# A two-layer trunk of mLSTM heads and RG-LRU: xb of group 1 ahead of the out chunks, weight sums begun behind casts, the LRU's z behind the head's y, and a background grant of 1.2

## The chip, the core and the metric

The kernel runs on one core of one Trainium2 chip. The metric is the device time of one execution in microseconds (us); the lower, the better. Before the change it is 1487.85, the median of three runs (1487.43 to 1488.35).

## The reference

Two layers, each x + [y_a, y_b] W_out with u = rms_norm(x), x of 256 rows and 2048 columns, everything float32:

```python
u = rms_norm(x, norm_g)
qk, v, o, z_a, ig, fg, xb, z_b = split(u @ w_in)
qk = silu(causal_dwconv(qk, qk_conv)); q, k = split(qk)        # 8 heads, dk 128, dv 256
h = mlstm_chunkwise(q, k, v, ig + i_bias, log_sigmoid(fg + f_bias)) * sigmoid(o)
y_a = head_norm(h) * head_norm_g * silu(z_a)
xc = causal_dwconv(xb, lru_conv_w) + lru_conv_b
y_b = rg_lru(xc, w_a, b_a, w_x, b_x, lam) * silu(z_b)          # h_t = a_t h_(t-1) + u_t
x = x + concat(y_a, y_b) @ w_out
```

After the second layer follows a final rms_norm. The products with w_in (2048 x 12304) and w_out (4096 x 2048) are nearly all of the work on the matrix engine.

## The kernel before

**Groups, items, halves.** Each layer is worked in four groups g of two mLSTM heads and 512 LRU channels. An item is one product of a group: "in" with a kind (qk, v, o, z for the heads, xb and zb for the LRU), "gate" (the LRU's two gates) or "out" (512 columns of the product of the group before with w_out). `_sequence` writes the order of the items by hand, one layer after the other and group by group; an item has 1 to 4 units of 1 MB of weights, and a unit two halves of 128 x 1024. In what follows a half is called by item and group, such as o2 or zb1. Two items of groups 2 and 3 (PAIR: z of group 2 and o of group 3) are not multiplied in this way but by seven products of blocks and sums of blocks, 28 smaller "block" halves to a layer, strewn between the others.

**A half.** float32 products are made of float32r pieces: `prepare` casts a raw half to wH on ACT and subtracts it on DVE, wL = raw - wH; then PE runs twelve matmuls of 512 columns (x high by wH, x high by wL, x low by wH; block halves run six). The main loop goes over the halves: it prepares half n + 3 (AHEAD), emits the matmuls of half n, and pumps background work. wH and wL have four buffers each, so that a cast waits for the matmuls of the half four before it.

**Background work.** All else is written as generators in the list bg: each yields the price of what it has emitted, or "wait" to let the turn pass. `pump` runs them in their order until the credit of the step is spent. The grant per half is a fixed number, and a greater one (2.6) when more than two generators, beside those put aside, are in the list. Such work is recorded with V (DVE) and S (ACT), whose instructions are ordered behind the splits (DVE: the split before the newest; ACT: the newest cast). All engines run their instructions in the order in which they were emitted, but the scheduler may move what is not ordered. The generators that the change touches:

- `qk_post` (the queries and keys of a group): the product is transposed on its way through memory (blk, moved on SP's queue, fr on POOL's queue), joined to ch on ACT, then a convolution of four taps on DVE and ACT (qc, 4 x 4 instructions), a sigmoid, a product, and the split qks. It then makes scores (Pt), ps_n, the head norm, and so on, in later generators.
- `e_gen`: nG (a row of the gates) is written to memory by `gates_gen`, and nb is read back as a broadcast; E is formed from nb in four DVE instructions.
- `xb_post`: the same transposition for xb; the convolution xc and its split xcs, which the gate item multiplies (ps_gt). `gate_post`: the LRU's gates and scan, which end in the key "lru".
- `zb_post`: the transposed z_b, its sigmoid, y_b and its split (ybH, ybL); for group 3 of layer 0 `zb_post_c` does it by channels with no transposition. "hz" means that head h and z have been combined, "yT" that the head's y stands transposed.
- `out_chunk`: for groups 0 to 2 a staged product that POOL's queue adds to x_d in memory (accumulating DMA, st["gq"]).
- `block_sums`: makes sums of x (sums, sum_t) and, in `moved`, sums of weight blocks in memory: w_d begins as a copy on SP's queue, and further blocks are added to it by accumulating DMAs on POOL's queue, PACE steps apart; `load_block` reads it as rawb.

**Queues.** SP's queue carries the loads raw and rawb, the moved transpositions and the first w_d copies. POOL's queue carries fr, nb, x_d and the w_d adds.

**Lines.** 112 is the wrapper through which V and S record; 395 is `mm_a` (products with x or y), 840 the gate's matmuls, 940 to 946 `zb_post_c`, 1093 the add to w_d, 516 fr, 637 nb, 1149 to 1151 the block products, 1410 the pump.

Of the kernel before, what the change touches and what calls it, by code (L numbers as in the profile page):

```python
# [20 lines left out]
DEPTH = 2  # L21
# [20 lines left out]
def _sequence():  # L42
# [6 lines left out]
    for l in range(DEPTH):  # L49
        for g in range(NG):  # L50
            fill = [("out", l, g - 1, c) for c in range(4)] if g > 0 else []
            head = {0: ("o", "qk", "v"), 1: ("qk", "o", "v"), 2: ("qk", "o", "v")}.get(g, ("o", "v", "qk"))
            items = [("in", l, k, g) for k in head]
            at = 0 if ("z", g) in PAIR else 2
            items += fill[0:at] + [("in", l, "xb", g)] + fill[at:4]
            items += [("in", l, "z", g), ("gate", l, g)]
            items.insert(len(items) if g > 0 else -2, ("in", l, "zb", g))
            us = [u for it in items for u in units(it)]
            if l > 0 and g == 0:
                us[0:8] = [us[i] for i in (0, 4, 1, 5, 2, 6, 3, 7)]  # L60
            seq += us
# [36 lines left out]
def tile_trunk(ctx, tc, x, xt, par, gw, gb, ws, final_g, out):  # L98
# [165 lines left out]
    def order(ins, prev):  # L264
        tc.add_manual_dep(ins.ins, prev.ins.name,
                          mybir.DependencyInfo(mybir.DependencyClass.NoSync, mybir.DependencyReason.DATA),
                          reason="an order of the program")

    bg, aside = deque(), []
# [416 lines left out]
    def qk_post(l, g, acc):  # L686
        bg.append(e_gen(l, g))
        fr = to_channels(l, acc)

        def gen():  # L690
            for _ in range(LANDING):
                yield "wait"
            ch = joined(fr)
            yield 0.3
            qc = work.tile([P, 4, T], F32, tag="c4", name="qc", bufs=2)
            sg = work.tile([P, 4, T], F32, tag="sC", name="qsg")
            for ct in range(4):
                conv(ch, qc, ct, O_QKW + 4 * (8 * (ct % 2) + 2 * g + ct // 2), l, None)
                yield 1.2
            order(S.activation(out=sg, in_=qc, func=AF.Sigmoid), st["wH"])  # L700
            tt_(qc, qc, sg, ALU.mult)
            yield 1.2
            while ("aT", l) not in st:
                yield "wait"
            q = work.tile([P, 4, 2, T], F32R, tag="xcs", name="qks")
            S.copy(out=q[:, :, 0, :], in_=qc)
            tt_(q[:, :, 1, :], qc, q.bitcast(F32)[:, :, 0, :], ALU.subtract)
            yield 1.2
            for _ in range(3):
# [140 lines left out]
    def gate_post(l, g):  # L850
        ending = (l, g) == (DEPTH - 1, NG - 1)

# [41 lines left out]
    def zb_post(l, g, acc):  # L894
# [3 lines left out]
        def gen():  # L898
            for _ in range(LANDING - 3 if ending else FAR):
                yield "wait"  # L900
            while ("lru", l, g) not in st or ("hz", l, g) not in st:
                yield "wait"
# [21 lines left out]
    def zb_post_c(l, g, acc, s_):  # L924
# [11 lines left out]
        def gen():  # L936
# [6 lines left out]
            yield 0.2  # L943
            S.copy(out=yH[:, sl_, :], in_=zb[:, sl_, :])
            tt_(yL[:, sl_, :], zb[:, sl_, :], yH.bitcast(F32)[:, sl_, :], ALU.subtract)
            if s_ == 1:
# [22 lines left out]
    def out_chunk(l, g, c):  # L969
# [9 lines left out]
        def postfn():  # L979
            ps = acc()  # L980
            if g < NG - 1:
                stage = act.tile([P, 2, 512], F32, tag="stage", name="stage")
                S.copy(out=stage, in_=ps)
                st["gq"] = G.dma_start(out=xd[c], in_=stage, accum_op=ALU.add)
                return
            if c == 0:
# [37 lines left out]
    def block_sums(l):  # L1024
# [5 lines left out]
        def made(i, key, negated, p, q, pieces=1, after=None):  # L1030
            to, n = sums[i], 8 // pieces
            for k in range(pieces):
# [13 lines left out]
                for f in (difference,  # L1046
# [7 lines left out]
                    yield 1.2 / pieces + 0.1  # L1054
                    yield "wait"
                    if pieces == 1:
                        yield "wait"
                if pieces == 4:
# [26 lines left out]
    def weight_sums():  # L1085

        def moved(l, to, start, r, c, j, h):
            cs = slice(1024 * h, 1024 * h + 1024)
            src = block_unit(l, r, c, j)[:, cs]
            if start:  # L1090
                order(nc.sync.dma_start(out=wd[l][to][j][:, cs], in_=src), st["ld"])
            else:
                order(G.dma_start(out=wd[l][to][j][:, cs], in_=src, accum_op=ALU.add), st["gq"])
            for _ in range(PACE[l]):
# [286 lines left out]
    for n, hf in enumerate(order_):  # L1381
# [27 lines left out]
        if "from" not in hf:  # L1409
            pump(1.05 if sum(g not in aside for g in bg) <= 2 else 2.6)  # L1410
    drain()
# [94 lines left out]
```

## Time and profile before

| | value |
|---|---|
| median of 3 runs | 1487.85 us |
| the profiled execution, its own time | 1487.9 us |
| its span | 1486.1 us |
| bytes moved | 383.43 MB, mean 258 GB/s |
| matmuls, VectorE, ScalarE instructions | 6782, 1564, 1226 |

The span is the time from the first to the last instruction of the profiled execution; the rest of its time lies around it. In a row of the timeline stand the start, the duration, the engine, the line, the operation, output<-inputs, and in brackets the idle time of the engine before it with what ended it. A DVE or ACT instruction overlaps the next by about 0.1 us, so that the step from one start to the next, not the duration, is what it takes of the engine.

### The profile page before, as it was taken

What the parts mean: (1) busy time and instruction counts of PE and PEld (TensorE: products, weight loads), DVE (VectorE), ACT (ScalarE), POOL (GpSimd) and SP (SyncE); (2) the same over time, 40 slices, a digit from 0 to 9 for tenths busy, and PEclk for the clock granted to TensorE, in tenths of its full rate; (3) what the DMA queues carried; (4) which work ended last, traced back from release to release, by engine and by line L of the source; (5) the groups of instructions that cost most, each with busy time, mean ns of one, the idle gap of its engine ahead of it and who ended that gap; (6) DMA issues with size and microseconds to landing.
All of it is one profiled execution on the core that took longest, in us unless ns stands there. A gap on an engine that the chain in (4) does not pass through costs nothing.

```text
span 1486.1 us, 18768 instructions
## 1 busy us (share of the span) xinstructions
PE 1471.3 (99%) x6782; PEld 1226.2 (83%) x6782; DVE 1144.3 (77%) x1564; ACT 957.4 (64%) x1226; POOL 110.4 (7%) x186
## 2 busy tenths in 40 slices
PE   9999999999999999999999999999999999999997
PEld 7888888888888888888888787888888888888886
DVE  5788987788777676778867789867888776766785
ACT  7666865567655765558665577755667567655675
POOL 0020000100100001000000100000001000010002
PEclk9999999999999999999999999999999999999999
DMA  9867899998987998985886667698698668677783
GB/s 338 322 205 253 264 340 270 295 285 251 314 266 255 273 303 268 288 276 213 278 285 191 216 203 244 239 263 268 224 282 287 226 226 241 234 242 262 237 276 116
DMA packets 104045, 383.43 MB, mean 258 GB/s; under 512 B 11392, under 2 KB 31888, under 8 KB 84496
## 3 DMA queue, kind: packets, MB, share of 16 engines
q1 hardware_dynamic: 87536, 327.41, 63.0%
q0 software_dynamic: 13952, 50.35, 15.5%
q10 hardware_dynamic: 2464, 4.47, 0.8%
q8 instruction: 53, 0.87, 0.2%
q14 instruction: 40, 0.33, 0.1%
HBM read 344.95 MB, written 62.41 MB: 274 GB/s over the span
## 4 chain that ended last, share of the span: by engine, by line
PE 87%; DVE 5%; issue 3%; ACT 2%; DMA 2%; SPq 0%; POOL 0%; DVEq 0%; POOLq 0%; ACTq 0%
PE acc L395 73%; PE ps_gt L840 3%; DVE wL L112 2%; PE ps_b L1149 1%; PE ps_b L1150 1%; PE ps_b L1151 1%; PE acc L408 1%; ACT wH L112 1%; PE acc L1248 1%; PE acc L1246 1%; PE acc L1247 1%; DVE gate L112 1%; ACT L112 1%; DVE xc L112 0%; PE ps_g L568 0%
## 5 line engine op out<-in xcount | busy, mean ns | idle before, releaser
L395 PE MATMUL acc<-wH,x_s 128*128 128x512 f32 x2752 | 860.6, 390 | 0.6 <-ACT wH L112 0.6
L112 DVE TENSOR_TENSOR wL<-raw,wH 128x1024 fp32r<-128x1024 f32 (+1 forms) x500 | 598.3, 1203 | 244.9 <-ACT wH L112 243.5
L112 ACT CAST wH<-raw 128x1024 fp32r<-128x1024 f32 (+1 forms) x500 | 514.8, 1037 | 368.6 <-PE acc L395 304.0
L395 PEld LDWEIGHTS acc<-wH,x_s 128*128 128x128 f32 x2752 | 516.1, 188 | 108.0 <-ACT wH L112 1.9
L395 PE MATMUL acc<-wL,x_s 128*128 128x512 f32 x1376 | 534.7, 390 | 3.7 <-DVE wL L112 3.7
L395 PEld LDWEIGHTS acc<-wL,x_s 128*128 128x128 f32 x1376 | 258.4, 188 | 57.9 <-DVE wL L112 5.1
L395 PE MATMUL acc<-wH,ybL 128*128 128x512 f32 x224 | 87.3, 390 | 0.7 <-DVE ybL L112 0.7
L395 PE MATMUL acc<-wH,ybH 128*128 128x512 f32 x224 | 87.3, 390 | 0.0
L395 PE MATMUL acc<-wL,yaH 128*128 128x512 f32 x224 | 87.2, 389 | 0.0
L395 PE MATMUL acc<-wH,yaH 128*128 128x512 f32 x224 | 87.2, 389 | 0.0
L395 PE MATMUL acc<-wH,yaL 128*128 128x512 f32 x224 | 87.1, 389 | 0.0
L395 PE MATMUL acc<-wL,ybH 128*128 128x512 f32 x224 | 87.0, 389 | 0.0
L112 ACT ACT_TABLE_LOAD x60 | 77.0, 1283 | 10.6 <-DVE qc L112 5.3
L112 DVE TENSOR_TENSOR wL<-rawb,wH 128x1024 fp32r<-128x1024 f32 x56 | 68.5, 1223 | 7.7 <-ACT wH L112 6.6
L112 ACT CAST wH<-rawb 128x1024 fp32r<-128x1024 f32 x56 | 59.0, 1053 | 21.2 <-PE acc L395 11.2
L516 POOL DMA_DIRECT2D fr<-moved x34 | 18.9, 557 | 518.3 <-DMA moved<-blk 343.7
L112 DVE SCALAR_TENSOR_TENSOR qc<-ch,pars,qc 128x255 f32<-128x255 f32 (+2 forms) x96 | 42.8, 479 | 11.1 <-ACT qc L112 10.4
L395 PEld LDWEIGHTS acc<-wH,ybL 128*128 128x128 f32 x224 | 42.1, 188 | 9.9 <-DVE ybL L112 1.1
L395 PEld LDWEIGHTS acc<-wH,yaH 128*128 128x128 f32 x224 | 42.1, 188 | 8.7
L395 PEld LDWEIGHTS acc<-wH,yaL 128*128 128x128 f32 x224 | 42.0, 188 | 8.7
L395 PEld LDWEIGHTS acc<-wL,yaH 128*128 128x128 f32 x224 | 42.1, 188 | 8.6
L395 PEld LDWEIGHTS acc<-wH,ybH 128*128 128x128 f32 x224 | 42.0, 188 | 8.5
(222 smaller groups left out, 1607.6 us busy)
## 6 DMA issues: line engine op xcount, KB each, us to landing
raw<-in_ws_dram SPq DMA_DIRECT2D x152, 1024.0 KB, 6.6
raw<-in_ws_dram SPq DMA_DIRECT2D x190, 512.0 KB, 5.9
fr<-moved POOLq DMA_DIRECT2D x34, 512.0 KB, 6.1
moved<-blk SPq DMA_DIRECT2D x132, 128.0 KB, 2.9
w_d<-in_ws_dram POOLq DMA_DIRECT2D x32, 512.0 KB, 9.9
rawb<-w_d SPq DMA_DIRECT2D x32, 512.0 KB, 6.2
rawb<-in_ws_dram SPq DMA_DIRECT2D x24, 512.0 KB, 6.2
x_d<-stage POOLq DMA_DIRECT2D x24, 512.0 KB, 7.2
```

The lines of the kernel that those rows point to most:

```text
L112: ins = f(*a, **k)
L395: st["mm"] = PE.matmul(o, a_[:, kt, P * t : P * t + P], W[:, k], start=b, stop=z)
L408: PE.matmul(ps[:, ct, T * part : 2 * T], W[:, k, P * ct : P * ct + P], moving, start=first and k == 0 and part == 0, stop=last and k == 3 ...
L516: i0 = back.dma_start(out=fr.rearrange("p a c t i -> p a (c t i)"), in_=moved)
L840: PE.matmul(o, W[:, ib, jl], xs[:, ib, a, :], start=j == 0 and i == 0 and W is Hv and a == 0, stop=i == 1 and W is Lv, skip_group_check=True)
L1149: PE.matmul(box["b"], aH, Hv[:, k], start=opening and k == 0, stop=False, skip_group_check=True)
L1150: PE.matmul(box["b"], aH, Lv[:, k], start=False, stop=False, skip_group_check=True)
L1151: PE.matmul(box["b"], aL, Hv[:, k], start=False, stop=kp == 3 and k == 1, skip_group_check=True)
L1246: PE.matmul(o, yH[:, kt, tsl], Hv[:, k, cs], start=start and k == 0, stop=False)
L1247: PE.matmul(o, yH[:, kt, tsl], Lv[:, k, cs], start=False, stop=False)
L1248: PE.matmul(o, yL[:, kt, tsl], Hv[:, k, cs], start=False, stop=stop and k == 1)
```

## The change

The order of items changes at one place: in group 1 of both layers xb now stands ahead of the four out chunks, where it stood between the second and the third (groups 0, 2 and 3 keep the place that they had). An add to w_d waits for the newest wH cast by a semaphore, and is not begun within two steps of an accumulate to x_d. `qk_post` marks that it is at work (st["turning"]), and in group 2 it lets three turns pass more. `zb_post` waits for "yT" where it waited for "hz", and for the end of "turning" (not in group 3, layer 1). `gate_post` of group 3 yields the smaller prices in both layers. The last two instructions of `zb_post_c` are recorded without the order behind the splits. In block_sums one "wait" is kept only for one kind of sum. The grant is 1.2 where it was 1.05.

```diff
--- before.py
+++ after.py
@@ -51,7 +51,7 @@
             fill = [("out", l, g - 1, c) for c in range(4)] if g > 0 else []
             head = {0: ("o", "qk", "v"), 1: ("qk", "o", "v"), 2: ("qk", "o", "v")}.get(g, ("o", "v", "qk"))
             items = [("in", l, k, g) for k in head]
-            at = 0 if ("z", g) in PAIR else 2
+            at = 2 if g == NG - 1 else 0
             items += fill[0:at] + [("in", l, "xb", g)] + fill[at:4]
             items += [("in", l, "z", g), ("gate", l, g)]
             items.insert(len(items) if g > 0 else -2, ("in", l, "zb", g))
@@ -265,6 +265,11 @@
         tc.add_manual_dep(ins.ins, prev.ins.name,
                           mybir.DependencyInfo(mybir.DependencyClass.NoSync, mybir.DependencyReason.DATA),
                           reason="an order of the program")
+
+    def paced(ins, prev):
+        tc.add_manual_dep(ins.ins, prev.ins.name,
+                          mybir.DependencyInfo(mybir.DependencyClass.Sync, mybir.DependencyReason.DATA),
+                          reason="a transfer begun behind it")
 
     bg, aside = deque(), []
     timed = []
@@ -686,10 +691,12 @@
     def qk_post(l, g, acc):
         bg.append(e_gen(l, g))
         fr = to_channels(l, acc)
+        relaxed = g == NG - 2
 
         def gen():
             for _ in range(LANDING):
                 yield "wait"
+            st["turning"] = True
             ch = joined(fr)
             yield 0.3
             qc = work.tile([P, 4, T], F32, tag="c4", name="qc", bufs=2)
@@ -697,14 +704,21 @@
             for ct in range(4):
                 conv(ch, qc, ct, O_QKW + 4 * (8 * (ct % 2) + 2 * g + ct // 2), l, None)
                 yield 1.2
+            if relaxed:
+                yield "wait"
             order(S.activation(out=sg, in_=qc, func=AF.Sigmoid), st["wH"])
+            if relaxed:
+                yield "wait"
             tt_(qc, qc, sg, ALU.mult)
             yield 1.2
+            if relaxed:
+                yield "wait"
             while ("aT", l) not in st:
                 yield "wait"
             q = work.tile([P, 4, 2, T], F32R, tag="xcs", name="qks")
             S.copy(out=q[:, :, 0, :], in_=qc)
             tt_(q[:, :, 1, :], qc, q.bitcast(F32)[:, :, 0, :], ALU.subtract)
+            st["turning"] = False
             yield 1.2
             for _ in range(3):
                 yield "wait"
@@ -848,7 +862,7 @@
         return f
 
     def gate_post(l, g):
-        ending = (l, g) == (DEPTH - 1, NG - 1)
+        ending = g == NG - 1
 
         def gen():
             while "sp" not in st:
@@ -898,7 +912,9 @@
         def gen():
             for _ in range(LANDING - 3 if ending else FAR):
                 yield "wait"
-            while ("lru", l, g) not in st or ("hz", l, g) not in st:
+            while ("lru", l, g) not in st or ("hz" if ending else "yT", l, g) not in st:
+                yield "wait"
+            while st["turning"]:
                 yield "wait"
             xc, _ = st["xc", l, g]
             sg = work.tile([P, 4, T], F32, tag="sE", name="zsg")
@@ -941,8 +957,9 @@
             yield 0.2
             nc.vector.tensor_tensor(out=zb[:, sl_, :], in0=sg, in1=xc[:, sl_, :], op=ALU.mult)
             yield 0.2
-            S.copy(out=yH[:, sl_, :], in_=zb[:, sl_, :])
-            tt_(yL[:, sl_, :], zb[:, sl_, :], yH.bitcast(F32)[:, sl_, :], ALU.subtract)
+            nc.scalar.copy(out=yH[:, sl_, :], in_=zb[:, sl_, :])
+            nc.vector.tensor_tensor(out=yL[:, sl_, :], in0=zb[:, sl_, :], in1=yH.bitcast(F32)[:, sl_, :],
+                                    op=ALU.subtract)
             if s_ == 1:
                 st["ybT", l, g] = True
             yield 0.6
@@ -982,6 +999,7 @@
                 stage = act.tile([P, 2, 512], F32, tag="stage", name="stage")
                 S.copy(out=stage, in_=ps)
                 st["gq"] = G.dma_start(out=xd[c], in_=stage, accum_op=ALU.add)
+                st["staged"] = st["n"]
                 return
             if c == 0:
                 new_ss()
@@ -1052,8 +1070,8 @@
                     if pieces == 4:
                         continue
                     yield 1.2 / pieces + 0.1
-                    yield "wait"
                     if pieces == 1:
+                        yield "wait"
                         yield "wait"
                 if pieces == 4:
                     yield 1.9
@@ -1087,10 +1105,14 @@
         def moved(l, to, start, r, c, j, h):
             cs = slice(1024 * h, 1024 * h + 1024)
             src = block_unit(l, r, c, j)[:, cs]
+            while not start and st["n"] - st.get("staged", -9) < 2:
+                yield "wait"
             if start:
                 order(nc.sync.dma_start(out=wd[l][to][j][:, cs], in_=src), st["ld"])
             else:
-                order(G.dma_start(out=wd[l][to][j][:, cs], in_=src, accum_op=ALU.add), st["gq"])
+                i0 = G.dma_start(out=wd[l][to][j][:, cs], in_=src, accum_op=ALU.add)
+                order(i0, st["gq"])
+                paced(i0, st["wH"])
             for _ in range(PACE[l]):
                 yield "wait"
 
@@ -1407,7 +1429,7 @@
         while timed and timed[0][0] <= n:
             timed.pop(0)[1]()
         if "from" not in hf:
-            pump(1.05 if sum(g not in aside for g in bg) <= 2 else 2.6)
+            pump(1.2 if sum(g not in aside for g in bg) <= 2 else 2.6)
     drain()
```

Both programs have the same instructions on every engine. What moves shows in the lists of DVE. Layer 1, group 0: the splits of the last half of xb0 and the first of zb0, with the convolution of the queries (qc) and E. Before:

```order
740 L112 TENSOR_TENSOR wL<-raw,wH 128x1024
741 L112 SCALAR_TENSOR_TENSOR qc<-ch,pars,qc 128x255
742 L112 SCALAR_TENSOR_TENSOR qc<-ch,pars,qc 128x254
743 L112 SCALAR_TENSOR_TENSOR qc<-ch,pars,qc 128x253
744 L112 TENSOR_SCALAR E<-nb,at_6974 128x256
745 L112 TENSOR_SCALAR E<-nb,at_6974 128x128
746 L112 TENSOR_SCALAR E<-nb,at_6974 128x256
747 L112 TENSOR_SCALAR E<-nb,at_6974 128x128
748 L112 TENSOR_TENSOR wL<-raw,wH 128x1024
```

After:

```order
733 L112 TENSOR_TENSOR wL<-raw,wH 128x1024
734 L112 SCALAR_TENSOR_TENSOR qc<-ch,pars,qc 128x254
735 L112 SCALAR_TENSOR_TENSOR qc<-ch,pars,qc 128x255
736 L112 SCALAR_TENSOR_TENSOR qc<-ch,pars,qc 128x253
737 L112 SCALAR_TENSOR_TENSOR qc<-ch,pars,qc 128x254
738 L112 TENSOR_TENSOR wL<-raw,wH 128x1024
739 L112 TENSOR_SCALAR E<-nb,at_6974 128x256
740 L112 TENSOR_SCALAR E<-nb,at_6974 128x128
741 L112 TENSOR_SCALAR E<-nb,at_6974 128x256
742 L112 TENSOR_SCALAR E<-nb,at_6974 128x128
743 L112 SCALAR_TENSOR_TENSOR qc<-ch,pars,qc 128x253
744 L112 SCALAR_TENSOR_TENSOR qc<-ch,pars,qc 128x255
```

E's four instructions stood ahead of zb0's first split (the second wL of the first list); now they stand behind it, and four qc stand ahead of it where three did.

Layer 0, group 2, at the end of o2, from the split of a block half (wL<-rawb) on; the wL behind it is that of o2's last half, and the one after that (behind the lists' ends) that of v2's first half. Before:

```order
413 L112 TENSOR_TENSOR wL<-rawb,wH 128x1024
414 L112 SCALAR_TENSOR_TENSOR qc<-ch,pars,qc 128x255 x2
415 L112 SCALAR_TENSOR_TENSOR qc<-ch,pars,qc 128x254 x2
416 L112 SCALAR_TENSOR_TENSOR qc<-ch,pars,qc 128x253 x2
417 L112 SCALAR_TENSOR_TENSOR qc<-ch,pars,qc 128x255
418 L112 TENSOR_TENSOR wL<-raw,wH 128x1024
419 L112 SCALAR_TENSOR_TENSOR qc<-ch,pars,qc 128x254
420 L112 SCALAR_TENSOR_TENSOR qc<-ch,pars,qc 128x253
```

After:

```order
394 L112 TENSOR_TENSOR wL<-rawb,wH 128x1024
395 L112 TENSOR_TENSOR ybL<-zb,ybH 128x512 x2
396 L112 TENSOR_SCALAR E<-nb,at_695 128x256
397 L112 TENSOR_SCALAR E<-nb,at_695 128x128
398 L112 TENSOR_SCALAR E<-nb,at_695 128x256
399 L112 TENSOR_SCALAR E<-nb,at_695 128x128
400 L112 TENSOR_TENSOR wL<-raw,wH 128x1024
401 L112 SCALAR_TENSOR_TENSOR qc<-ch,pars,qc 128x255 x2
402 L112 SCALAR_TENSOR_TENSOR qc<-ch,pars,qc 128x254 x2
403 L112 SCALAR_TENSOR_TENSOR qc<-ch,pars,qc 128x253 x2
```

Seven qc stood ahead of the split of o2's last half; now ybL and E stand there, and the qc come behind it, six of them ahead of v2's first split.

Layer 1, the end of z1, the two gate halves and zb1's first half (xc is the LRU's convolution, sum_t and sums belong to the sums of x, xcs is the split of xc). Before:

```order
968 L112 TENSOR_TENSOR wL<-raw,wH 128x1024
969 L112 SCALAR_TENSOR_TENSOR xc<-ch,pars,xc 128x255
970 L112 TENSOR_TENSOR sums_6985<-res,sums_6985 128x512
971 L112 SCALAR_TENSOR_TENSOR xc<-ch,pars,xc 128x254
972 L112 SCALAR_TENSOR_TENSOR xc<-ch,pars,xc 128x253
973 L112 TENSOR_TENSOR wL<-raw,wH 128x1024 x2
974 L112 SCALAR_TENSOR_TENSOR xc<-ch,pars,xc 128x255
975 L112 TENSOR_TENSOR sum_t<-x_s 128x256
976 L112 SCALAR_TENSOR_TENSOR xc<-ch,pars,xc 128x254
977 L112 TENSOR_TENSOR sum_t<-sum_t,x_s 128x256
978 L112 SCALAR_TENSOR_TENSOR xc<-ch,pars,xc 128x253
979 L112 TENSOR_TENSOR sum_t<-sum_t,x_s 128x256
980 L112 TENSOR_TENSOR wL<-raw,wH 128x1024
```

After:

```order
953 L112 SCALAR_TENSOR_TENSOR xc<-ch,pars,xc 128x255
954 L112 SCALAR_TENSOR_TENSOR xc<-ch,pars,xc 128x254
955 L112 SCALAR_TENSOR_TENSOR xc<-ch,pars,xc 128x253
956 L112 TENSOR_TENSOR wL<-raw,wH 128x1024
957 L112 TENSOR_TENSOR sum_t<-x_s 128x256
958 L112 TENSOR_TENSOR sum_t<-sum_t,x_s 128x256 x2
959 L112 CAST sums_6985<-sum_t 128x256
960 L112 TENSOR_TENSOR wL<-raw,wH 128x1024
961 L112 TENSOR_TENSOR sums_6985<-sum_t,sums_6985 128x256
962 L112 TENSOR_TENSOR xcs<-xc,xcs 128x2x256
963 L112 TENSOR_TENSOR wL<-raw,wH 128x1024 x2
964 L112 TENSOR_TENSOR xcs<-xc,xcs 128x2x256
965 L112 SCALAR_TENSOR_TENSOR za<-acc,rstd,sz 128x512
```

Of the three wL behind the xc in the first list, the double one is that of the gate, and the last that of zb1: two times three xc stood among them. Now xc is done ahead of z1's last split, and between the gate's first split and zb1's only the end of the sums and one xcs are left.

## The prediction

> **What bounds the kernel now.** The page comes first: busy time, then the slices.
>
> ```profile
> span 1486.1 us, 18768 instructions
> PE 1471.3 (99%) x6782; PEld 1226.2 (83%) x6782; DVE 1144.3 (77%) x1564; ACT 957.4 (64%) x1226; POOL 110.4 (7%) x186
> PE   9999999999999999999999999999999999999997
> PEclk9999999999999999999999999999999999999999
> ```
>
> TensorE is full at full clock. The change removes no instruction, so only time in which PE stands still can go. The table by windows says where that is (window, its length, PE busy, ...).
>
> ```profile
> 320.00:420.00 100.00, 99.42 (x461) 82.61 (x460) 84.72 (x111) 70.32 (x89) 8.64 (x14) 1.00 0.86 279
> 420.00:700.00 280.00, 280.00 (x1335) 235.69 (x1334) 205.53 (x271) 180.60 (x227) 20.00 (x28) 1.00 0.85 268
> ...
> 830.00:930.00 100.00, 97.73 (x461) 80.91 (x460) 87.25 (x126) 70.34 (x93) 5.38 (x11) 1.00 0.66 221
> 1060.00:1080.00 20.00, 18.82 (x106) 16.25 (x105) 18.28 (x28) 15.96 (x23) 0.00 (x0) 1.00 0.57 195
> ```
>
> The stretch from 420 to 700 stands for those I leave out: PE never stops there. PE's waits over the whole run name the releasers (total, times, longest).
>
> ```profile
> PE acc L395 <- DVE wL L112: 3.7, 4, 1.2
> PE acc L395 <- DVE ybL L112: 0.7, 1, 0.7
> PE acc L395 <- ACT wH L112: 0.6, 2, 0.3
> ```
>
> So PE waits for late splits of weights: VectorE's wL and, once, its ybL. Those are the places where background work on DVE or ACT stands ahead of a split. What one bracketed wait costs shows at the third of them:
>
> ```profile
> 915.67 0.39 PE L395 MATMUL acc<-wH,x_s 128*128 128x512 f32 x1
> 917.06 0.50 PE L395 MATMUL acc<-wL,x_s 128*128 128x512 f32 x1 [1.00 <-DVE wL L112]
> 917.40 0.64 PE L395 MATMUL acc<-wH,x_s 128*128 128x512 f32 x2
> ```
>
> Matmuls overlap: undisturbed, one begins some 0.23 us after the other (a pair lasts 0.64, one 0.39 to 0.41), and twelve make a half unit of 2.72. From 915.67 to 917.06 are 1.39, so 1.16 are lost, and 0.34 to the next start is another 0.11: a bracket of 1.00 costs 1.27. I charge each bracket plus 0.27.
>
> **The change part by part.** The sum is made against the profiled execution: span 1486.1, its own time 1487.9, which is the median 1487.85 within 0.1.
>
> *Grants of 1.2 instead of 1.05, and L1's first query turn.* Around 840 (DVE, ACT, PE):
>
> ```profile
> 830.07 1.01 DVE L112 TENSOR_SCALAR E<-nb,at 128x256 f32<-128x256 f32 x4 [3.91 <-DMA nb<-nG_d]
> 830.99 1.22 DVE L112 TENSOR_TENSOR wL<-raw,wH 128x1024 fp32r<-128x1024 f32 x1
> 834.33 1.94 DVE L112 SCALAR_TENSOR_TENSOR qc<-ch,pars,qc 128x253 f32<-128x253 f32 x4
> 836.35 1.28 ACT L112 ACT_TABLE_LOAD   x1 [2.09 <-DVE qc L112]
> 839.75 1.04 ACT L112 CAST wH<-raw 128x1024 fp32r<-128x1024 f32 x1
> 841.06 1.18 DVE L112 TENSOR_TENSOR wL<-raw,wH 128x1024 fp32r<-128x1024 f32 x1
> 840.84 0.50 PE L395 MATMUL acc<-wH,x_s 128*128 128x512 f32 x1 [0.25 <-ACT wH L112]
> 842.29 0.50 PE L395 MATMUL acc<-wL,x_s 128*128 128x512 f32 x1 [0.95 <-DVE wL L112]
> ```
>
> DVE stands 3.91 us before E because nb, a round trip through memory, lands late; the split behind E and all convolution steps (qc) shift with it, the sigmoid waits for the last qc, and one cast and one split for that. Here 0.25 + 0.16 and 0.95 + 0.27 are lost, 1.6, with the slow pair behind the first 1.7. In the new order a split and two more qc stand ahead of E. The nG chain has two qc in it, so nb lands some 0.7 later, 830.8. Then E 0.92, two qc 0.9, split 1.13, two qc 1.0: the last qc ends at 834.8, where it ended at 836.3. Shifting the cast by 1.4 gives 838.3, in time for 840.4; the split 839.6 to 840.8, where PE needs it at 840.65. So 0.2 + 0.27 at worst stay: **minus 1.3**, from 0 (nb another 1.4 late) to 1.7.
>
> *Waits of the query turn (g 2), and the background that moves with them.* Layer 0, near 403:
>
> ```profile
> 399.39 2.86 DVE L112 SCALAR_TENSOR_TENSOR qc<-ch,pars,qc 128x255 f32<-128x255 f32 x7 [3.61 <-ACT qc L112]
> 402.16 1.22 DVE L112 TENSOR_TENSOR wL<-raw,wH 128x1024 fp32r<-128x1024 f32 x1
> 403.44 0.50 PE L395 MATMUL acc<-wL,x_s 128*128 128x512 f32 x1 [0.52 <-DVE wL L112]
> ```
>
> Seven qc stand ahead of a split and wait 3.61 us for the transposed queries (fr) to land. Now that split stands ahead of them and only the next, needed a half (2.7 us) later, stands behind six: 399.4 + 6 × 0.4 + 1.2 = 403.0 against some 405.7. That is **minus 0.8**, down to 0 where fr lands 2.7 later.
>
> *LRU z behind the head's y.* Layer 1, ahead of 917.06:
>
> ```profile
> 912.32 1.22 DVE L112 TENSOR_TENSOR zb<-zb,zsg 128x1024 f32<-128x1024 f32 x1
> 913.46 1.25 DVE L112 STREAM_TRANSPOSE blk<-tok 128x1024 f32<-128x1024 f32 x1
> 914.62 1.25 DVE L112 TENSOR_TENSOR ybL<-zb,ybH 128x512 fp32r<-128x512 f32 x2
> 915.79 2.36 DVE L112 TENSOR_TENSOR wL<-raw,wH 128x1024 fp32r<-128x1024 f32 x2
> ```
>
> From one begin to the next the zb product takes 1.14, the transposition 1.16, the two ybL 1.17; a first zb product of the same size, one split earlier, another 1.14: 4.6 ahead of the late split. In the new order the second product and ybL go behind later splits, and yaL, of the size of zb, comes ahead: 1.14 + 1.16 + 1.14 = 3.4. The split comes 1.2 earlier, where 1.16 were lost: **minus 1.1**, from 0, if yaL waits for its cast on ACT, to 1.27.
>
> *The second group's xb ahead of the out chunks.* Layer 1, at gate and zb of group 1:
>
> ```profile
> 1062.91 0.48 DVE L112 SCALAR_TENSOR_TENSOR xc<-ch,pars,xc 128x255 f32<-128x255 f32 x1
> 1065.10 1.22 DVE L112 TENSOR_TENSOR wL<-raw,wH 128x1024 fp32r<-128x1024 f32 x1
> 1066.37 0.50 PE L395 MATMUL acc<-wL,x_s 128*128 128x512 f32 x1 [1.18 <-DVE wL L112]
> ```
>
> The last convolution steps of xb1 and sums of x, 2.2 us from 1062.91 to 1065.10, hold this split. In the new order xb's convolution is done before the gate's splits, and only xcs stands near: **minus 1.45** (1.18 + 0.27), to 0 if fr of xb1 were late; it has 17 halves to land, where it had 13 or 14. Layer 0 has the same order and a pause of 0.3 by the starts of the gate's matmuls near 329; with the same cause gone, **minus 0.3**. The out chunks themselves move behind xb: their x_d accumulates on POOL's queue stand four halves, 10.9 us, apart,
>
> ```profile
> x_d<-stage POOLq DMA_DIRECT2D x24, 512.0 KB, 7.2
> w_d<-in_ws_dram POOLq DMA_DIRECT2D x32, 512.0 KB, 9.9
> 303.38 2.04 POOL L1093 DMA_DIRECT2D w_d<-in_ws_dram  x2
> 368.86 0.38 SPq L337 DMA_DIRECT2D rawb<-w_d  x1
> ```
>
> and land in 7.2: nil.
>
> *Pacing.* An add of a w_d waits on the cast wH emitted last, and lets two steps pass after an accumulate. Behind it on POOL wait fr, nb and the x_d accumulates, at most one cast (2.7 us). Its reader in layer 0 begins at 368.86, 65 us after the last adds at 303.38; six adds each 2.7 later and 9.9 to land are 26. I take nil, from minus 0.5 (fr landing with fewer transfers beside it) to plus 1.0 (one fr behind a waiting add). The Trainium skill, "DMA: Bandwidth & Descriptors", Rules for kernel authors, says to begin a transfer early and wait for it late, and so speaks against beginning these behind a cast; by it alone an add whose reader is near would cost its landing. No reader is that near here.
>
> *zb's last copies without the order, gate_post's smaller credits, one wait less in block_sums.* The place they touch is the end of layer 0:
>
> ```profile
> 708.34 0.69 DVE L112 TENSOR_TENSOR ybL<-zb,ybH 128x512 fp32r<-128x512 f32 x1
> 709.08 0.50 PE L395 MATMUL acc<-wH,ybL 128*128 128x512 f32 x1 [0.67 <-DVE ybL L112]
> ```
>
> In the order two splits still stand directly ahead of this ybL, and zb waits for a copy that ACT makes behind a table load: I leave 0.94 where it is (nil, from minus 0.94).
>
> *A new wait.* E of layer 0, group 0:
>
> ```profile
> 87.46 1.01 DVE L112 TENSOR_SCALAR E<-nb,at 128x256 f32<-128x256 f32 x4 [2.10 <-DMA nb<-nG_d]
> 88.78 1.21 DVE L112 TENSOR_TENSOR wL<-raw,wH 128x1024 fp32r<-128x1024 f32 x1
> ```
>
> A further qc comes into the nG chain (nb 0.4 later) and another between E and the split (0.4): its end goes from 90.0 to 90.8, and 90.6 is when the twelve matmuls reach it by their 2.72 a half. **Plus 0.3**, from 0 to 1.0.
>
> Sum: 1.3 + 0.8 + 1.1 + 1.45 + 0.3 − 0.3 = 4.65. Shorter pauses near 873 and 885 (the window from 830 to 930 has 0.07 idle beside its three brackets of 2.2; by the starts of matmuls 0.5) go with the earlier head products in the new order: 5.15. The bounds: all six brackets (6.5 by the rule) and the small pauses gone are 7.0, time 1480.8; half of the sum given back in new waits 1485.3.
>
> **Rivals.**
> *Moved, not removed* (saves 1 to 4, about 1485.5). DVE's total stays 1144.3, and E's wait, fr's landing and table loads are the same; each sum above ends within 0.2 to 1 us of the need, so the next split may be the late one. For: two of the six places depend on a transfer's landing. Against: the window from 420 to 700 goes through the same work of group 2 and 3 without a pause.
>
> *It doesn't do what it says* (1487.9). The grants' rise would be eaten by the generators' own prices and xb1's transfer be late anyway. Against: the order has xc ahead of the gate's splits.
>
> *Slower* (about 1495): generators that wait for y and for the query turn pile up, more than two count, and the grant is 2.6 rather than 1.2. Then DVE owes 1.13 + 2.6 = 3.7 per half of 2.72, a deficit of 1.0. Four buffers let a split be three halves ahead, 3 × 2.72 − 2 × 1.13 = 5.9 us; from the seventh such half in a row on, PE waits. Twelve in a row in groups 2 of both layers are 2 × (12 − 5.9) = 12, less 5.15: 1494.9. The new order shows two or three halves in a row with so much between splits, then a gap; so it is improbable. The Trainium skill, "TensorE: Matmul & The Clock Gate", Part 1, says the clock halves after an idle window of about 3.4 us, which would add to it; every bracket here is at most 1.18, and PEclk stays at 9, so nothing here shows it.
>
> **How the numbers follow.** Forecast 1487.85 − 5.15 = 1482.7, rounded up to **1482.8**, chance 0.62; moved 0.22, of which a quarter saves over 3; does nothing 0.07; beyond the floor 0.02; slower 0.07. A measurement of this kernel can tell some 0.2%, 3.0 us: under 1484.9 is faster. Faster 0.62 + 0.02 + 0.06 = 0.70, same 0.23, slower 0.07. The range 1480.8 to 1486.8 takes in the forecast and the moved case and leaves out under 2 in 10.
>
> **What would show it.** PE's waits for wL after: from four to at most one or two, each below 0.4. At 403, 917 and 1066 no bracket; DVE's E in layer 1 behind a split, and still a bracket for ybL near 705. Windows 320 to 420 and 1060 to 1080 at full PE. Wrong if a new bracket of over 0.5 stands one or two halves behind an old place, if fr or nb land later than by 1 us, or if a run of halves shows DVE full for 20 us.

## The result, and the profile after

The changed kernel takes 1484.39 us, the median of 18 runs (1483.09 to 1487.12); the kernel before, in as many runs beside it, 1487.84. The ratio is 0.9978, with a 95% interval of 0.9971 to 0.9984: some 3.3 us faster, about 0.2%. Forecast were 1482.8 and a range from 1480.8 to 1486.8. The profiled execution took 1483.76.

The page of the changed kernel, and the table by windows at the places shown of before (window, its length, PE busy, ...):

```profile
span 1482.1 us, 18794 instructions
PE 1470.0 (99%) x6782; PEld 1226.2 (83%) x6782; DVE 1142.5 (77%) x1564; ACT 956.1 (65%) x1226; POOL 112.2 (8%) x186
...
PEclk9999999999999999999999999999999999999999
...
10.00:320.00 310.00, 309.29 (x1409) 256.70 (x1408) 251.93 (x389) 201.33 (x266) 26.45 (x44) 1.00 0.88 289
320.00:420.00 100.00, 100.00 (x466) 83.79 (x465) 81.79 (x100) 70.99 (x90) 8.83 (x15) 1.00 0.89 283
...
830.00:930.00 100.00, 99.81 (x475) 83.70 (x474) 86.86 (x127) 71.58 (x93) 6.13 (x11) 1.00 0.69 235
...
1060.00:1080.00 20.00, 20.00 (x113) 17.52 (x112) 15.54 (x19) 17.42 (x28) 0.56 (x1) 1.00 0.76 237
```

The engines' work is that of before (DVE 1142.5 against 1144.3). The windows from 320 to 420, 830 to 930 and 1060 to 1080 are now full or nearly so; they lacked 0.58, 2.27 and 1.18. The window from 10 to 320, which was full, now lacks 0.71. PE's waits in the changed kernel (total, times, longest):

```profile
PE acc L400 <- DVE ybL L961: 0.7, 1, 0.7
PE acc L400 <- ACT wH L112: 0.5, 1, 0.5
PE acc L400 <- DVE wL L112: 0.4, 1, 0.4
PE ps_S L734 <- DVE Pt L112: 0.3, 1, 0.3
PE acc_x L1268 <- ACT w_own L112: 0.3, 1, 0.3
PE ps_n L663 <- DVE hh L112: 0.2, 1, 0.2
```

Waits for wL went from four of 3.7 to one of 0.4; the one for ybL is still there; those for Pt, w_own and hh are new to the view (0.3 was lost at hh's place before too, with no wait for hh in the view). Where the waits for wL and Pt stand (DVE, then PE):

```profile
87.97 1.01 DVE L112 TENSOR_SCALAR E<-nb,at 128x256 f32<-128x256 f32 x4 [2.40 <-DMA nb<-nG_d]
89.68 1.22 DVE L112 TENSOR_TENSOR wL<-raw,wH 128x1024 fp32r<-128x1024 f32 x1
90.95 0.50 PE L400 MATMUL acc<-wL,x_s 128*128 128x512 f32 x1 [0.39 <-DVE wL L112]
...
103.22 2.32 DVE L112 TENSOR_TENSOR wL<-raw,wH 128x1024 fp32r<-128x1024 f32 x2
105.46 0.61 DVE L112 TENSOR_TENSOR Pt<-ps_S,Pt 128x256 f32<-128x256 f32 x2
105.93 0.39 PE L734 MATMUL ps_S<-qks 128*128 128x256 f32 x1 [0.31 <-DVE Pt L112]
```

E waits for nb, and the split two qc behind it ends 0.5 too late, as foreseen (0.7 instead of 0.3 by the starts). The scores' second product waits until Pt has read a bank of PSUM (ps_S), and Pt stands behind two splits: 0.6, not foreseen; with the greater grant the scores are emitted one half earlier than before.

A pause is measured by the starts of the matmuls: what a step from one start to the next takes beyond its usual length, 0.23 us for 512 columns. So measured, PE lost 7.0 us outside of the first 10 us before, and 3.4 now. Gone: 1.7 near 840, 1.46 near 1066, 1.28 near 917, 0.79 near 403, 0.33 near 329, 0.2 of small ones. Come: 0.67 near 91, 0.64 near 106, 0.66 around 1452, 0.1 at 866. By the two totals that is 3.6; with the first 10 us (0.25 less) and pauses below 0.06 it makes the 4.0 between the two spans.

### The profile page after: what moved, and what is told of

It reads as the page before. It is cut to its first block, busy times and chain, and to the rows that moved or that the text cites. A ratio compares the mean times of both kernels' runs of the same rounds, so it can differ in the third digit from the quotient of the medians.

```text
span 1482.1 us, 18794 instructions
## 1 busy us (share of the span) xinstructions
PE 1470.0 (99%) x6782; PEld 1226.2 (83%) x6782; DVE 1142.5 (77%) x1564; ACT 956.1 (65%) x1226; POOL 112.2 (8%) x186
## 4 chain that ended last, share of the span: by engine, by line
PE 88%; DVE 2%; ACT 1%; DMA 1%; issue 1%; SPq 0%; DVEq 0%; ACTq 0%
PE acc L400 75%; PE ps_gt L854 3%; PE ps_b L1171 2%; PE ps_b L1172 2%; PE ps_b L1173 2%; PE acc L413 1%; DVE wL L112 1%; DMA moved<-blk 1%; DMA fr<-moved 0%; DVE xc L112 0%; PE ps_n L663 0%; PE ps_n L665 0%; PE ps_S L734 0%; PE ps_n L664 0%; PE acc L1270 0%
## 5 line engine op out<-in xcount | busy, mean ns | idle before, releaser
L112 DVE SCALAR_TENSOR_TENSOR qc<-ch,pars,qc 128x253 f32<-128x253 f32 (+2 forms) x96 | 42.4, 477 | 9.4 <-ACT qc L112 9.1
L400 PEld LDWEIGHTS acc<-wL,ybH 128*128 128x128 f32 x224 | 42.1, 188 | 8.7
```

The costliest lines, as they stand in the source:

```text
L112: ins = f(*a, **k)
L400: st["mm"] = PE.matmul(o, a_[:, kt, P * t : P * t + P], W[:, k], start=b, stop=z)
```

## The experiments

The changed kernel was run again, then with one part undone or altered; two parts were put alone into the kernel before, and the kernel before was profiled once more. A place is named by its time in the first profiles.

**e1: the changed kernel again.** No edit.

> The changed kernel again, on another occasion. Theory: what it lost is fixed by its order: pauses of 0.5 to 0.7 us near 91 (wL behind E), 106 (ps_S behind Pt) and 709 (ybL) come back, near 1453 (w_own, behind a sigmoid that waits for fr) 0.5 comes back if the order makes it; time 1484.4. Rival: these are chance of that one execution's transfers: the pause near 1453 is gone or another place has it, time 1482.5 to 1484.

Measured 1484.13 (1482.77 to 1484.58), ratio 0.9969 (0.9956 to 0.9981). Its profile has 91 (0.63), 106 (0.58) and 709 (0.94) again, the pause at 1453 not, and 0.7 near 49 and 0.3 near 12 that the first one has not. So the first three belong to the order. A pause near 49, of 0.2 to 1.0, stands in ten of the twelve later profiles, those of e9 and e10 (the kernel before) among them; it is not the change's. The one at 1453 was behind a transfer, in the first profile of the changed kernel (ACT):

```profile
1444.10 1.28 ACT L112 ACT_TABLE_LOAD   x1
1447.17 1.06 ACT L112 ACTIVATE zsg<-fr 128x1024 f32<-128x1024 f32 x1 [1.78 <-DMA fr<-moved]
1449.83 1.14 ACT L112 CAST ybH<-zb 128x512 fp32r<-128x512 f32 x2 [1.60 <-DVE zb L112]
1450.87 2.94 ACT L112 CAST w_own<-raw 128x1024 fp32r<-128x1024 f32 x3
```

In the new order this sigmoid stands one cast earlier, ahead of three w_own casts instead of two, and holds them when fr lands late, here by 1.78.

**e2: the grant left at 1.05.**

```diff
-            pump(1.2 if sum(g not in aside for g in bg) <= 2 else 2.6)
+            pump(1.05 if sum(g not in aside for g in bg) <= 2 else 2.6)
```

> The change with the grant left at 1.05. Theory (each pause belongs to an order of DVE that depends on several parts together): the pauses near 91, 106 and 1453 go (1.8 in the changed kernel's profile), and two come back: near 403 (seven qc stand ahead of o2's last split again, 0.8) and near 840 (E ahead of zb0's first split again, 1.7); 1484.4 + 0.7 = 1485.1. Rival (the grant alone made the gain): all six old pauses are back, 1487.8.

Measured 1488.08 (1485.96 to 1491.07), ratio 1.0000 (0.9991 to 1.0009): the rival's time, but not by its mechanism. Of the old large pauses only 840 (1.4) is back; 403, 709 and 917 are gone, and at the gates of group 1 stand new and larger ones, 1.0 and 0.6 near 330, 0.45 and 2.2 near 1066 to 1071. Its DVE and PE there:

```profile
1061.97 1.51 DVE L112 SCALAR_TENSOR_TENSOR xc<-ch,pars,xc 128x255 f32<-128x255 f32 x3
1069.98 0.69 DVE L112 TENSOR_TENSOR xcs<-xc,xcs 128x512 fp32r<-128x512 f32 x1
1070.72 0.38 PE L854 MATMUL ps_gt<-xcs,wH 128*128 128x256 f32 x1 [1.90 <-DVE xcs L112]
```

With the other parts in place and the small grant, xb's convolution is run so late that the gate's matmuls wait for it, although xb itself is computed early (e8, below, has the small grant without the other parts and no such wait; which of them delays it was not tried). In the changed kernel the last xc of that item ends at 1053, ahead of the gate's splits.

The profiled execution took 1486.88, 1.2 under the median, so its pauses are not all of the time. In five of the eleven runs the mean granted clock was 0.997, in the six others 0.998, and the five have a median of 1489.3, the six of 1487.1. One stretch at half clock, as e11 shows it below, lowers the mean by 0.0012 (an estimate: half of 3.41 us in 1487). So such stretches are probably a part of e2's time; no profile of one of those five runs was kept.

**e3: group 1's xb put back behind two out chunks.**

```diff
-            at = 2 if g == NG - 1 else 0
+            at = 0 if ("z", g) in PAIR else 2
```

> The change with group 1's xb left behind two of the out chunks. Theory: xc stands among the gate's splits again, so the pauses near 329 (0.3) and 1066 (1.46) come back, and the order of layer 0 is moved so far that seven qc stand ahead of o2's last split (403: 0.8); 840 and 917 stay gone: 1484.4 + 2.6 = 1487.0. Rival (the prediction's split of the parts): 403 belongs to the query turn's waits and stays gone: 1486.2.

Measured 1490.49 (1488.52 to 1492.18), ratio 1.0014 (1.0005 to 1.0023): slower than the kernel before, and 3.5 and 4.3 above what the two theories made of it. 1.0 at 1071 is back; near 330 PE loses 4.5 in one place (the last row is a window, as in the table above: length, PE busy, ..., clock, DMA share, GB/s):

```profile
329.12 1.04 ACT L112 CAST wH<-raw 128x1024 fp32r<-128x1024 f32 x1 [4.42 <-DMA raw<-in_ws_dram]
330.21 0.49 PE L400 MATMUL acc<-wH,x_s 128*128 128x512 f32 x1 [1.67 <-ACT wH L112]
331.48 0.80 PE L400 MATMUL acc<-wL,x_s 128*128 128x512 f32 x1 [0.77 <-DVE wL L112]
331.40:334.80 3.40, 3.33 (x8) 2.65 (x9) 3.29 (x7) 3.39 (x6) 0.00 (x0) 0.50 0.32 130
```

A cast waits 4.42 us for a load of weights, and behind the two waits the clock falls to half: of the 4.5, the waits are 3.0 by the rule of a bracket plus 0.27, the clock the other 1.5. The load took 12.6 us from its issue to its landing; in the changed kernel the same load took 6.7. An add to w_d was issued 1.4 behind it, where the changed kernel has one 5.4 behind; but e5 has one 1.2 behind, and there the load took 7.0. So why it lands late stays open. 403 stays gone, though seven qc stand ahead of that split again.

**e4: 1.05 at the two ends.**

```diff
-            pump(1.2 if sum(g not in aside for g in bg) <= 2 else 2.6)
+            pump((1.05 if n < 40 or n > 530 else 1.2) if sum(g not in aside for g in bg) <= 2 else 2.6)
```

> The change with the grant of 1.05 over the first 40 halves and after half 530, 1.2 between. Theory: the new pauses near 91, 106 and 1453 come from the greater grant at the two ends and go, all else stays: 1484.4 - 1.8 = 1482.6. Rival (they are chance of the transfers): 1484.4 with pauses elsewhere.

Measured 1482.66 (1482.22 to 1483.64), ratio 0.9962 (0.9950 to 0.9975). Beside the wait at its very start, PE has two left:

```profile
PE acc L400 <- DVE ybL L961: 0.7, 1, 0.7
PE ps_n L663 <- DVE hh L112: 0.2, 1, 0.2
```

91 and 106 are gone, so they were the grant's price in the first turn; e10, below, has them with the grant alone. The five runs overlap with those of the changed kernel beside them (e1).

**e5: zb_post waits for "hz" again.**

```diff
-            while ("lru", l, g) not in st or ("hz" if ending else "yT", l, g) not in st:
+            while ("lru", l, g) not in st or ("hz", l, g) not in st:
```

> The change with zb_post waiting for the head (hz) again instead of for its y. Theory: zb's second product, the transposition and ybL stand ahead of o1's split again, so 1.28 comes back near 917 and nothing else: 1484.3 + 1.3 = 1485.6. Rival: the part also orders layer 0, where seven qc stand ahead of o2's last split again, and 403 comes back with 0.8: 1486.4.

Measured 1484.78 (1483.96 to 1486.76), ratio 0.9978 (0.9969 to 0.9986). 917 is back with 0.74, where it was 1.28, and nothing stands at 403. e10, the grant alone, has 0.74 there too: so with both parts the grant takes 0.54 of the 1.28, and the wait for y the rest. In the times the part is worth 0.4 to 0.7, which the intervals do not separate from nothing.

**e6: no pacing.**

```diff
-            while not start and st["n"] - st.get("staged", -9) < 2:
-                yield "wait"
...
-                paced(i0, st["wH"])
```

> The change without the pacing: adds to w_d wait for no cast and for no accumulate. The order on DVE and ACT is nearly that of the changed kernel, so this is a clean test of the transfers. Theory: nil, 1484.3 within 0.5. Rival: the pacing kept the adds off fr, nb and the accumulates; without it fr lands later, and a pause of 0.5 to 1 us stands near 403 or at zb: 1485.3.

Measured 1484.24 (1483.18 to 1485.34), ratio 0.9979 (0.9970 to 0.9988): nil. Its profile has 91, 106 and 709 as the changed kernel, and 0.8 near 618 that e12 has with 0.3 and e10 with 0.6. The adds to w_d do land later without the pacing, in 9.9 (median) against 8.8 and 9.4 in the two profiles of the changed kernel, and x_d's accumulates earlier, in 7.2 against 8.1 and 7.8; the times show neither.

**e7: 1.05 also over the end of layer 0.**

```diff
-            pump(1.2 if sum(g not in aside for g in bg) <= 2 else 2.6)
+            pump((1.05 if n < 40 or n > 530 or 236 <= n < 272 else 1.2) if sum(g not in aside for g in bg) <= 2 else 2.6)
```

> The grant of 1.05 over the first 40 halves, halves 236 to 271 (the end of layer 0) and after 530; 1.2 elsewhere. In the order ybL stands between the two splits at the end of layer 0 instead of behind both, as it does with 1.05 throughout, where the pause near 709 was gone. Theory: 1482.7 - 0.9 = 1481.7. Rival: ybL waits for ybH on ACT, so the pause stays: 1482.7.

Measured 1481.81 (1481.25 to 1482.10), ratio 0.9960 (0.9947 to 0.9972), the fastest of all. All five runs lie below the lowest of the 23 of the changed kernel (1482.77) and below the lowest of e4 (1482.22). They were made on another occasion than those, but the kernel before differed by 0.2 and 0.3 only between them: 1487.54 here, 1487.74 beside e4, 1487.84 beside the first. Against its own kernel before e7 has no better ratio than e4 that the intervals would show; that 709 is gone is shown by its profile. First the changed kernel at the end of layer 0 (DVE, then PE), then this one (DVE):

```profile
705.76 2.35 DVE L112 TENSOR_TENSOR wL<-raw,wH 128x1024 fp32r<-128x1024 f32 x2
708.03 0.69 DVE L961 TENSOR_TENSOR ybL<-zb,ybH 128x512 fp32r<-128x512 f32 x1
708.77 0.50 PE L400 MATMUL acc<-wH,ybL 128*128 128x512 f32 x1 [0.67 <-DVE ybL L961]
```

```profile
705.19 1.22 DVE L112 TENSOR_TENSOR wL<-raw,wH 128x1024 fp32r<-128x1024 f32 x1
706.33 0.69 DVE L961 TENSOR_TENSOR ybL<-zb,ybH 128x512 fp32r<-128x512 f32 x1
706.93 1.22 DVE L112 TENSOR_TENSOR wL<-raw,wH 128x1024 fp32r<-128x1024 f32 x1
```

ybL stands between the two splits instead of behind both, and PE does not stop: its waits for it are gone from the view.

**e8: the move of xb alone, in the kernel before.**

```diff
-            at = 0 if ("z", g) in PAIR else 2
+            at = 2 if g == NG - 1 else 0
```

> The kernel before with group 1's xb moved ahead of the out chunks, nothing else. Theory (each part takes away its own pause, as the prediction had it): 329 and 1066 go, 1.8, the other four stay: 1487.8 - 1.8 = 1486.0. Rival (the parts work only together, as undoing either the grant or the move took more than its share): under the small grant xb's convolution ends late and the gate's matmuls wait for xcs near 329 and 1070, 2 to 3 us: 1488 or more.

Measured 1485.38 (1483.29 to 1487.61), ratio 0.9986 (0.9977 to 0.9995). 329 and 1066 are gone, with the small grant too; 709, 917 and a part of 840 (0.6) stay, and 403 is gone as well. The place of the small pauses near 871 has 0.6 instead of 0.3, and 0.25 stands near 1059. The profiled execution, 1484.18, is 1.2 under the median.

**e9: the kernel before, profiled again.** No edit; one run, 1487.53.

> The kernel before, a second profile. Theory: pauses that an order on DVE makes by itself come back at their size (709: 0.95, 917: 1.28, 1066: 1.46); those behind a transfer's landing (403 behind fr, 840 behind nb) differ by half a microsecond or more. Rival: all six are the same within 0.1.

709 (0.94), 917 (1.27) and 1066 (1.46) are the same within 0.02; 840 is 1.33 instead of 1.75, 329 is 0.5 with 0.3 just ahead, 0.5 has come near 540 and 0.4 near 49, and 403 is not there. The order is the same; the transfer is not. First the first profile of before, then the second, then that of e11 (POOL's issue of fr, SP's of the next load, raw, ACT's copy of fr, DVE's first qc):

```profile
391.24 0.55 POOL L516 DMA_DIRECT2D fr<-moved  x1 [8.87 <-DMA moved<-blk]
391.47 0.35 SPq L331 DMA_DIRECT2D raw<-in_ws_dram  x1
397.77 1.05 ACT L112 COPY ch<-fr 128x1024 f32<-128x1024 f32 x1 [3.46 <-DMA fr<-moved]
```

```profile
391.70 0.55 POOL L516 DMA_DIRECT2D fr<-moved  x1 [8.93 <-DMA moved<-blk]
392.15 0.35 SPq L331 DMA_DIRECT2D raw<-in_ws_dram  x1
395.30 1.05 ACT L112 COPY ch<-fr 128x1024 f32<-128x1024 f32 x1 [0.20 <-DMA fr<-moved]
396.93 2.86 DVE L112 SCALAR_TENSOR_TENSOR qc<-ch,pars,qc 128x255 f32<-128x255 f32 x7 [0.38 <-ACT qc L112]
```

```profile
392.70 0.35 SPq L336 DMA_DIRECT2D raw<-in_ws_dram  x1
393.06 0.56 POOL L521 DMA_DIRECT2D fr<-moved  x1 [14.84 <-DMA moved<-blk]
401.39 1.05 ACT L112 COPY ch<-fr 128x1024 f32<-128x1024 f32 x1 [3.12 <-DMA fr<-moved]
```

From issue to copy 6.5, 3.6 and 8.3 us. This is not mere scatter: it goes with how long before its neighbour raw fr is issued. In eleven of the fourteen profiles raw is issued 0.4 us or more behind fr, and fr lands 3.4 to 5.0 after its issue; raw 0.2 behind (the first profile of before) goes with 6.5, raw at the same time (e10) with 8.0, raw 0.4 ahead (e11) with 8.3. No run moved one of the two alone, so this is read from the profiles and not shown by an experiment.

**e10: the grant alone, in the kernel before.**

```diff
-            pump(1.05 if sum(g not in aside for g in bg) <= 2 else 2.6)
+            pump(1.2 if sum(g not in aside for g in bg) <= 2 else 2.6)
```

> The kernel before with the grant of 1.2, nothing else. Theory: the greater grant takes 840 away (1.7) and brings the pauses near 91 and 106 (1.2); 709 and 917 stay; at 329 and 1066 the convolution of xb ends late still: 1487.3. Rival (its undoing cost 3.9, so it is worth about that): 1484.

Measured 1488.60 (1487.27 to 1491.41), ratio 1.0010 (1.0001 to 1.0019): no gain, rather a loss of some 1.2. 840 and 1066 are gone, 917 has 0.74, 91 and 106 come, 333 has 1.3 (a wait for the gate), 622 has 0.6, 755 has 1.8, 713 1.35, and the convolution behind fr, which lands 8.0 after its issue, costs 2.6 near 405 to 408: 403 again, three times as large. The profile is that of the slowest of its runs, 1491.41, so the sizes near 405 and 755 are those of that execution.

**e11: without the three turns in group 2.**

```diff
-        relaxed = g == NG - 2
+        relaxed = False
```

> The change without the three more turns that qk_post lets pass in group 2. Theory: o2's last split keeps its place ahead of the qc, so these turns are not what took 403 away: nil there, 1484.3 within 0.6. Rival (the prediction): 403 is back with 0.8, 1485.1.

Measured 1483.99 (1482.77 to 1487.21), ratio 0.9975 (0.9965 to 0.9985): nil. The profiled execution was the slowest, 1487.21, and its extra 3 us stand at one place (DVE, PE, and two windows):

```profile
405.02 2.52 DVE L112 SCALAR_TENSOR_TENSOR qc<-ch,pars,qc 128x255 f32<-128x255 f32 x6 [4.37 <-ACT qc L112]
407.47 1.21 DVE L112 TENSOR_TENSOR wL<-raw,wH 128x1024 fp32r<-128x1024 f32 x1
408.74 0.69 PE L400 MATMUL acc<-wL,x_s 128*128 128x512 f32 x1 [1.85 <-DVE wL L112]
409.23 1.06 PE L400 MATMUL acc<-wH,x_s 128*128 128x512 f32 x2
...
405.00:408.70 3.70, 1.89 (x9) 1.21 (x7) 3.67 (x8) 3.70 (x6) 1.09 (x3) 1.00 0.77 323
408.90:412.30 3.40, 3.40 (x9) 2.66 (x10) 3.40 (x6) 3.37 (x5) 0.00 (x0) 0.50 0.31 67
```

It has the changed kernel's order there, six qc behind o2's last split and ahead of v2's first. fr came 8.3 after its issue, and the pause of 403 came back one half later, with 3.7 by the starts. The wait itself is 2.1 of it (1.85 + 0.27). The other 1.6 are the clock: from 408.87 the granted clock is 0.50 for 3.41 us, and a pair of matmuls takes 1.06 instead of 0.62 to 0.64. It is the only such drop in this profile between its start and its end; e3 has one, the other twelve profiles none. The run's mean clock is 0.997, that of the ten others 0.998 or 0.999.

**e12: the one wait of block_sums as it was.**

```diff
-                    if pieces == 1:
-                        yield "wait"
+                    yield "wait"
+                    if pieces == 1:
                         yield "wait"
```

> The change with the one wait of block_sums as it was. Theory: seven qc stand ahead of o2's last split again, but their fr lands early enough there (as it did where the grant or hz was undone), so no pause near 403: 1484.3 within 0.6. Rival: 403 is back, 0.8: 1485.1.

Measured 1484.64 (1483.47 to 1486.56), ratio 0.9981 (0.9971 to 0.9990): nil within its runs. Nothing stands at 403; 0.8 stands near 332.

## Why the prediction was right, and where it was not

**What bounds it** held: no instruction went, PE's clock and work stayed, and the gain is the pauses' own.

**840, the grant** (minus 1.3): all of the 1.7 went. The rows of the changed kernel (DVE):

```profile
829.83 1.01 DVE L112 TENSOR_SCALAR E<-nb,at 128x256 f32<-128x256 f32 x4 [2.50 <-DMA nb<-nG_d]
838.49 1.18 DVE L112 TENSOR_TENSOR wL<-raw,wH 128x1024 fp32r<-128x1024 f32 x1
```

E waited 2.50 for nb instead of 3.91, since it began to wait behind a split and two more qc, and the late split began at 838.49 instead of 841.06. nb landed by 829.83, not at the 830.8 that I allowed for two more qc in its chain. e2 (840 is back) and e10 (it is gone) show that the grant does it.

**917, z behind y** (minus 1.1): 1.28 went; e5 brings 0.74 of it back. The grant alone takes the other 0.54 (e10), and the wait for y takes all of it at the small grant (e2): the two overlap. The sum had yaL ahead of the split; in the new order yaL stands two splits earlier, at 906.43, and only the transposition and one zb product stand there.

**1066 and 329, xb earlier** (minus 1.75): 1.79 went; e8 shows that the move alone does it; at 1066 the grant alone does it too (e10), at 329 it does not.

**403, the query turn's waits** (minus 0.8): the pause was gone in the profile, but the step was wrong. e11 takes those waits out and o2's last split keeps its place and the kernel its time; it is other parts that keep the qc behind it (undoing the grant, the move of xb, the wait for y or the one in block_sums, each alone, puts seven qc ahead of it again: e2, e3, e5, e12). And those four have no pause there, nor has the second profile of the kernel before: 0.79 was what fr's landing cost in one execution. The changed order does not take the pause away. It moves the qc behind one split, which gives fr a half, 2.7 us, more; but it also puts a table load and E's activation between the copy of fr and the first qc (ACT, then DVE):

```profile
398.16 1.05 ACT L112 COPY ch<-fr 128x1024 f32<-128x1024 f32 x1 [0.37 <-DVE ybL L112]
399.23 1.28 ACT L112 ACT_TABLE_LOAD   x1
400.52 0.85 ACT L112 ACTIVATE E<-E 128x768 f32<-128x768 f32 x1
...
404.24 1.21 DVE L112 TENSOR_TENSOR wL<-raw,wH 128x1024 fp32r<-128x1024 f32 x1
```

From the copy to the split behind the qc are 6.1 us here; in the kernel before they were 4.4 (397.77 to 402.16). So 1.7 of the 2.7 are taken back, and fr may land about 1.0 later than before (an estimate from these rows), not 2.7 as the prediction allowed. In e11 it landed later than that, and the pause is there. In the two profiles of the changed kernel fr took 3.6 and 4.9, and none is there.

**709** (nil): still 0.94. The order's two splits ahead of ybL were rightly read as the cause; e7 puts one behind it and the pause goes. The copy on ACT that the prediction names beside them was not it: in the kernel before ybH had ended at 706.81, 1.5 us before ybL began.

**The new wait at 91** (plus 0.3): 0.67 and 0.63. The term was too small by half: the split ended at 90.90, where I had 90.8, and PE came to it at some 90.4, where I had 90.6, since it had lost 0.25 less at the start. **106** (0.6) was not seen at all: the greater grant brings the scores one half forward, and I looked only at what stands ahead of splits, not at banks that work behind splits empties. **The small pauses** (minus 0.5): 885 went, the one at ps_n stayed (0.3 before, 0.43 after).

In the named pauses the profile has 3.6 of the 5.15 forecast. The missing 1.55 is, within 0.1, 106 (0.64), 91 (0.37), the small pauses (0.44) and the place around 1452 (0.66), less some 0.6 by which 840 and 917 gave more. That the forecast stood within 2 us of the result is in part luck: 0.8 of its gain was a landing that the kernel before did not have in its second profile, and errors of both signs stand in the sum. The spans differ by 4.0, 0.4 more, through the first 10 us (0.25) and pauses too short to name. That the medians differ by 3.45 and not 4.0 is the changed kernel's profiled execution, 0.6 under its median. Runs in which fr comes late, as in e11, may be among the slower ones; no profile of the changed kernel shows one.

**The rivals.** "Moved, not removed" holds in part: 1.3 of what went came back near 91 and 106, through the grant. "Slower" did not come: no pauses over successive halves stand in the changed kernel's profile. But e2 and e3 show that the change with one part missing is as slow as before or slower, by another mechanism than the rival's: in e2 the work for the gates comes late, in e3 a load of weights does, and in e3 (in e2 probably) the clock falls behind the wait. The prediction had set a fall of the clock aside, as every bracket then known was 1.18 at most; the 3.4 us of idle time that it quotes for such a fall were not needed here: e11 has it behind a bracket of 1.85, e3 behind 1.67 and 0.77 close together. Brackets of 1.79 (e10) and 1.90 (e2) have none in their profiles, so the length alone does not decide it. The parts do not add: the move of xb alone gives 2.2, the grant alone costs some 1.2, all together give 3.4, and all without the grant nothing. That I priced each by its own pause and added them came near enough for all together and for the move of xb (1.75 against 2.2); for the grant it had the wrong sign (e10), and for leaving one part out it was far off (e2, e3).

Pacing was taken as nil, and e6 shows neither a loss nor a gain from it (0.15 from the changed kernel's median).

## What to carry to other kernels

In a kernel that one engine fills, a background grant is no dial for the whole run: the same 1.2 that took 1.7 off at one place cost 1.3 at another, and giving each stretch its own value (1482.7, then 1481.8) got more than the uniform change. Before a pause behind a transfer is put down to an order, profile the same kernel a second time: the three pauses made by the order came back within 0.02 us, while of those behind a landing one went from 0.8 to nothing and one from 1.7 to 1.3. Then look at which transfers were issued just beside the late one. And where splits for later halves are moved forward past other work, list everything that work frees too (banks, buffers), not only what stands in line.

## What the runs showed of the hardware that was not expected

The landing of a 512 KB transfer varied by more than any term of the sum, and in step with a neighbour: fr near 391 took 3.4 to 5.0 us where SP's next load was issued 0.4 us or more behind it (eleven profiles), 6.5 where 0.2 behind, 8.0 and 8.3 where at the same time or 0.4 ahead. In the kernel before, 0.2 us between two issues thus went with 2.9 us in the landing (6.5 against 3.6).

A wait well under 2 us can be followed by a halved clock: 0.50 for 3.41 us in e11, behind a wait of 1.85, and in e3, behind waits of 1.67 and 0.77. It cost 1.6 and 1.5 us more, nearly as much as the wait. Waits of 1.79 and 1.90 passed without it in the profiles of e10 and e2. So a single late landing could cost 3.7 us of PE in a kernel whose other pauses together were 3.4.

Pacing the accumulating transfers behind casts made the median landing of these 0.5 to 1.1 us earlier (e6) and changed nothing in the times.
